# Decayed cumulative sum of a matrix product: the start of the kernel and the engine orders of its first 42 slots

## The chip, the cores and the metric

One Trainium2 chip, one of its cores. The metric is the device time of one execution in microseconds (us); nine runs of the kernel before are at hand, and one execution taken by the hardware profiler.

## The reference

`x` is 16 x 2048 x 1024, `w` 1024 x 1024 and `decay` 1024 long, all float32.

```python
def reference(x, w, decay):
    B, S, D = x.shape
    xw = x @ w
    out = np.zeros_like(xw)
    out[:, 0, :] = xw[:, 0, :].copy()
    for t in range(1, S):
        out[:, t, :] = decay[None, :] * out[:, t - 1, :] + xw[:, t, :]
    return out.astype(np.float32)
```

So there is a matrix product, and behind it, for each of the 1024 columns, a first-order recurrence along time.

## The kernel before

**Tiles and slots.** Time is cut into 64 chunks of 512 steps, four to a batch. Two chunks make a group, and the 1024 columns of `w` make 8 blocks of 128. A *slot* is one block for one group: an output of 128 columns x 1024 steps, with the columns on the partitions, made by 16 matmuls (8 parts `k` of the sum, 2 chunks) of 128 x 512 in bfloat16. The last group is run as single chunks, so there are 31 x 8 + 2 x 8 = 264 slots. The outputs lie in PSUM in a ring of three buffers `ps` (1024 float32 each) and two of half the size, `spare` and `spare1`. Slots 0 to 3 are made together, chunk 0 first, then chunk 1, in the three `ps` and the two spares (lines 547 to 564); the others one after the other (lines 567 to 594).

**Loading x.** A chunk comes as four DMAs, one for each quarter of the partitions, that GpSimd (POOL) issues and that turn float32 into bfloat16 on the way, into one of four `xb` buffers (`load`, line 101). Chunks 0 and 1 come in halves of 256 steps, four DMAs each (`load_half`; letters M0 to M3). The rest stand in the list `loads`, from which each letter L takes one; chunk c + 4 is put there when chunk c is turned.

**Turning x.** VectorE (DVE) transposes a chunk in blocks of 32 x 32, two bfloat16 at a time (`turn`, line 110; T, or its halves t and u; E for the eight pieces of chunks 0 and 1), into one of two `xw`. ScalarE (ACT) sorts the pairs apart into one of five `xt` (`part`, line 119; X and Y are the halves of a chunk). In chunks 0 and 1 there are pieces of a quarter of the sum and half the time, done by VectorE (F) or ScalarE (G).

**Loading w.** `w` comes in quarters (h, e): h is the half of the columns, e the even or odd rows. They land in `stage`, which lies in the two output buffers not needed yet, and are copied into `wsb` in eight pieces of two quarters for each h: `settle`, W on VectorE, w on ScalarE. W0 and W1 are k = 0 and 2, W2 and W3 k = 4 and 6, W4 to W7 the odd k of h = 0; W8 to W15 are h = 1. Quarter (0, 0) is loaded as float32 by SyncE's queue in two parts, at the very start and again at line 317 behind the decays. The others come by POOL's queue as bfloat16: U1, U2 and U3. The 8 DMAs in flight on a queue each have a semaphore of their own, and a ninth waits for the first of them.

**The recurrence of a slot.** There are two ways (`Tile`, line 136). *Unpaired*: VectorE scans all 1024 steps straight from PSUM (S, line 216). *Paired*: ScalarE copies the output out of PSUM (`copy`) and scales its odd-placed steps by the decay (`odd`), POOL adds them in (`join`), VectorE scans 512 steps with the squared decay (S, line 196), ScalarE scales that result (`even`) and POOL adds the rest (`fill`). In both the result `so` is transposed back by VectorE (B, line 253) into an output buffer `ot`, which SyncE stores when four slots are in it. P is copy, odd, zero and join together (p, g, z, j are the parts); C is even, fill and the saving of the last step (h, c, k). A slot's `ps` is free after its `odd` if paired, after its S if not. A slot is unpaired when its block n is 3 or 7, except that `flips` turns the choice round; with the list of before slots 0, 2, 3, 8, 11, 13, 16, 20, 21, 23, 25, 30, 32 and 39 of the first 42 are unpaired.

**What sets the order.** Each engine works through its instructions in the order of the program. That order is written out by hand as letters: `agenda[-99]` is the start, `agenda[s]` what is put behind the matmuls of slot s. For a slot with no entry `usual(s)` makes the order: P of s, S of s - 1, S of s if it is unpaired, C of s - 1, B of s - 2 (or s - 1), then the T, X and Y that `later` has for this slot, then one or two L. `later` puts T, X and Y of an odd chunk 7, 6 and 4 slots ahead of its first slot, of an even one 11, 10 and 8. In the kernel before, slots 0 to 41 and the last 20 are written out, and `usual` serves the 200 or so between. T14 and X13, Y13 are the first that come from `later`.

**Slots 8 and 9.** Chunk 2 is used ahead of chunk 3: step 8 makes both slots, chunk 2 of each and then chunk 3 of each (lines 577 to 585).

Before the first work on x, 27 matmuls of zeros run on TensorE (line 308).

Of the kernel before, what the change touches and what calls it, by code (L numbers as in the profile page):

```python
# [10 lines left out]
BF16 = mybir.dt.bfloat16  # L11
# [14 lines left out]
def kernel(  # L26
# [26 lines left out]
    nc = tc.nc  # L53
    pin = tc.keep_in_program_order
    B, S, D = x.shape
# [5 lines left out]
    K = CQ // P  # L61
    M = K // 2
    TL = 512
    NJ = TL // P
    NC = S // TL
    R = K // 2
# [32 lines left out]
    xt_of = {}  # L99
# [10 lines left out]
    def turn(c, j0=0, j1=NJ, m0=0, m1=M):  # L110
        if c not in xw_of:
            xw_of[c] = ring(sb, "xw", 2, [128, M, NJ, P, 2], BF16)
        src = xb_of[c][:, j0:j1].rearrange("p j c -> p (j c)").bitcast(FP32)
        dst = xw_of[c].rearrange("p m j i e -> p (m j i e)").bitcast(FP32)
        pin(nc.vector.transpose(  # L115
            out=dst.rearrange("p (m j i) -> p j m i", m=M, i=P)[:, j0:j1, m0:m1],
            in_=src.rearrange("p (j m c) -> p j m c", m=M, c=P)[:, :, m0:m1]))
# [143 lines left out]
    class Outlet:  # L261
# [7 lines left out]
        def store(self, b, t0):  # L269
# [3 lines left out]
            for i, q in enumerate((0, 2, 1, 3)):  # L273
# [7 lines left out]
    room = [ot_tile(2 * NJ).rearrange("p j c -> p (j c)") for _ in range(2)]  # L281
    size = M * CH
    stage = {(0, 0, 0): room[0][:, 0:size // 2],
             (0, 0, M // 2): room[0][:, size // 2:size],
             (0, 1, 0): room[0][:, size:size * 3 // 2].bitcast(BF16),
             (1, 0, 0): room[1][:, 0:size // 2].bitcast(BF16),
             (1, 1, 0): room[1][:, size // 2:size].bitcast(BF16)}
# [1 line left out]
    def load_w(queue, h, e, m0=0, m1=M):  # L289
        for q in range(NQ):  # L290
            pin(queue.dma_start(  # L291
                out=stage[h, e, m0][quad(q)].rearrange("p (m d) -> p m d", m=m1 - m0),
                in_=_ap(w, [[2 * D, P], [2 * P * D, m1 - m0], [1, CH]],
                        (q * CQ + m0 * 2 * P + e) * D + h * CH)))
# [18 lines left out]
    for q in range(NQ):  # L313
        pin(nc.sync.dma_start(
            out=rows[q * P:q * P + R],
            in_=_ap(decay, [[P, R], [CH, 2], [1, P]], q * CR)))
    load_w(nc.sync, 0, 0, M // 2, M)
    cols = const.tile([128, 2, P], FP32, name="cols")

    def load_half(i):  # L320
# [65 lines left out]
    slots += [([c], n) for c in groups[-1] for n in range(K)]  # L386
    tiles = []

    def turn_half(half):
        def act(c):  # L390
            if half == 0:
                turn(c, 0, NJ, 0, 2)
            else:
                turn_and_load(c, 2)
        return act

    def turn_and_load(c, m0=0):
        turn(c, 0, NJ, m0, M)
        if 2 <= c < nch - 4:
            loads.extend((c + 4, q) for q in range(NQ))  # L400

# [4 lines left out]
        "C": lambda s: tiles[s % len(slots)].complete(),  # L406
        "B": lambda s: tiles[s % len(slots)].back(),
        "T": turn_and_load,
        "t": turn_half(0),
        "u": turn_half(1),  # L410
        "X": lambda c: part(c, nc.scalar.copy, 0, 2),
        "Y": lambda c: part(c, nc.scalar.copy, 2, M),
        "x": lambda c: part(c, nc.vector.tensor_copy, 0, 2),
# [21 lines left out]
        "L": lambda i: load(*loads.pop(0)) if loads else None,  # L435
    }
    agenda = {
        -99: "M0 M1 U1 M2 M3 U2 U3 W0 w1 D W2 w3 E1 E0 G2 G3 F1 F0 E2 E3 G4 G5 F7 F6 W6 w7 W4 W5 E5 E4 G10 F11 G9 F8 E6 E7 L G12 F13 L G15 F14",
        0: "L W9 w11 L W8 W10 L",
        1: "S0 L",  # L440
        2: "L p1 z1",
        3: "L w13 S2 w15 k0 L w14 w12 g1",
        4: "L B0 k2 j1 B2 p4 L S1 L g4",
        5: "j4 t2 k1 h1 u2 L X2 c1 S3 Y2 z4 L",
        6: "L L B1 k3 p5 B3 p6 z5 z6 L",
        7: "g6 S4 g5 L j6 t3 h4 k4 u3 c4 X3 S6 L Y3 L T4 j5 h6 k6 p7 S5 z7 c6 g7",
        8: "",
        9: "d B4 k5 h5 j7",
        10: "X4 B6 c5 S8 Y4 L B5",
        11: "p9 L p10 S7 g9 B8 h7 j9 g10 T5",  # L450
        12: "k7 z9 c7 z10 j10 B7 X5 L S9",
        13: "L p12 S11 L h9 z12 Y5 c9 S10",
        14: "L g12 B11 h10 j12 B9 L S12 c10",
        15: "p14 S13 g14 L h12 j14 B10 c12",
        16: "p15 B13 L g15 B12 z14 z15 j15 S14 L",
        17: "S15 h14 c14 S16 h15 c15",
        18: "p17 B14 z17 L g17 L B15 k16 j17 B16",
        19: "z18 p18 S17 g18 T6 h17 j18 k17 c17",
        20: "T7 p19 z19 L g19 L X6 L B17 j19",
        21: "X7 S18 L S20 Y7 L S19",  # L460
        22: "k20 h18 k18 L Y6 S21 c18 k19 h19 B20 L",
        23: "k21 p22 c19 B18 g22 j22 B19 z22 L B21",
        24: "S22 S23 z24 k22 h22 c22",
        25: "p24 T8 k23 g24 j24 B23 X8 L",
        26: "L B22 L Y8 L S25 z26",
        27: "z27 p26 S24 g26 B25 h24 j26 T9 c24",
        28: "p27 g27 B24 L X9 j27 S26",
        29: "z28 L z29 p28 S27 L g28 L T10 h26 j28 Y9 c26",
        30: "S28 X10 B26 Y10 T11",
        31: "h28 S30 p29 c28 g29 h27 j29",  # L470
        32: "B28 X11 c27 S29 Y11 B30 B27",
        33: "p31 T12 g31 z31 h29 j31 c29 S32 X12",
        34: "p33 B29 g33 B32 k32 z33 Y12 j33",
        35: "S31 p34 z34 S33 h31 T13 h33 c31",
        36: "g34 k33 j34 p35 B31 g35 c33 S34",
        37: "j35 p36 B33 h34 z35 z36 S35 k34 g36 c34 k35 h35 j36 B34",
        38: "p37 z37 c35 S36 g37 j37 h36 B35 k36",
        39: "c36 p38 S37 g38 z38 B36 k37 h37 j38 c37 S38",
        40: "S39 h38 k38 c38 B37 p40 g40 z40 j40 k39 B38 B39 L L",
        41: "p41 g41 z41 j41 S40 h40 c40 L L",  # L480
        -20: "z-20",
        -19: "p-20 g-20",
        -18: "j-20 S-19 S-20 k-19 B-19",
# [15 lines left out]
        -2: "S-3 S-4",  # L499
        -1: "S-2 h-4 c-4 a-1 b-1 V",  # L500
    }
    flips = (0, 2, 7, 8, 13, 15, 16, 19, 20, 21, 25, 27, 30, 31, 32, 35, -19, -18, -16, -11, -8, -6, -3, -2)
    later = {}
    begun = {"T": 14, "X": 13, "Y": 13}
    for c in range(5, nch):
        first = c // 2 * K
        ahead = (7, 6, 4) if c % 2 else (11, 10, 8)
        for letter, a in zip("TXY", ahead):
            if c >= begun[letter]:
                later.setdefault(first - a, []).append(f"{letter}{c}")  # L510

    def usual(s):
        paired = [t.paired for t in tiles]
# [25 lines left out]
    for step, (g, n) in enumerate(slots):  # L539
        T = TL * len(g)  # L540
        left = step - len(slots)
        if n % R == 0:
            ns, nj = range(n, n + R), T // P
            outlets = [Outlet(ns, nj)]
        if left == -R:
            outlets = []
        if step == 0:
            heads = [ring(psp, "ps", 3, [128, T]) for _ in range(3)]
            firsts = [ps[:, 0:TL] for ps in heads] + [spares[0]]
            seconds = [ps[:, TL:T] for ps in heads] + [spares[1]]  # L550
            for j0, j1 in halves:
                for k in (0, 2, 4, 6):
                    for i in range(R):
                        matmul(firsts[i], i, k, xt_of[0], j0 * P, j1 * P)
            for k in (1, 3, 5, 7):
                for i in range(R):
                    matmul(firsts[i], i, k, xt_of[0])
            for k0 in range(0, K, 4):
                for i in range(R):
                    for k in range(k0, k0 + 4):  # L560
                        matmul(seconds[i], i, k, xt_of[1], 0, H * P)
            for i in range(R):
                for k in range(K):
                    matmul(seconds[i], i, k, xt_of[1], H * P, TL, H * P)
        if step < R:
            ps = heads[n] if n < 3 else tuple(spares)
        else:
            if step == K + 1:
                ps = nexts
            elif len(g) == 2 or n % R < 3:  # L570
                ps = ring(psp, "ps", 3, [128, T])
            else:
                ps = ring(psp, "spare", 1, [128, TL])
            todo = [(k, l) for k in range(K) for l in range(len(g))]
            if step < K:
                todo.sort(key=lambda kl: kl[0] % 2)
            elif step == K:
                todo = []
                nexts = ring(psp, "ps", 3, [128, T])
                for l in range(len(g)):  # L580
                    for i, both in enumerate((ps, nexts)):
                        for k in range(K):
                            matmul(both[:, l * TL:(l + 1) * TL], n + i, k, xt_of[g[l]])
            elif step == K + 1:
                todo = []
            if left == -1:
                ps = tuple(both[:, t:t + TL // 2] for t, both in zip(
                    (0, TL // 2), (ps, ring(psp, "ps", 3, [128, TL]))))
                for t, half in zip((0, TL // 2), ps):
                    for k in range(K):  # L590
                        matmul(half, n, k, xt_of[g[0]], t, t + TL // 2, t)
                todo = []
            for k, l in todo:
                matmul(ps[:, l * TL:(l + 1) * TL], n, k, xt_of[g[l]])
        tiles.append(Tile(g, n, ps, outlets))
        do = agenda.get(step, agenda.get(left) if left >= -20 else None)
        if do is None:
            do = usual(step)
        else:
            do = do.split()  # L600
            if left == -20:
                do = rest(step) + do
        perform(do)
# [29 lines left out]
```

## Time and profile before

| | |
|---|---|
| median of 9 runs | 913.1 us (912.2 to 913.79) |
| the profiled execution, its own time | 913.1 us |
| its span, first to last instruction | 911.2 us |
| TensorE (PE) busy | 897.7 us, 4195 matmuls |
| VectorE (DVE) busy | 831.0 us |
| ScalarE (ACT) busy | 675.7 us |
| GpSimd (POOL) busy | 649.2 us |
| mean granted clock of TensorE | 0.996 |
| one scan of 1024 steps from PSUM (L216) | 2261 ns, with the state of the group before 2321 ns |
| one scan of 512 steps (L196) | 1198 to 1280 ns |
| one transposition back (L253) | 1217 ns |
| one chunk turned (L115) | 2284 ns |
| half a chunk sorted (L123) | 1903 ns |
| copy, odd, even (L178, L164) | 1012, 693, 774 ns |
| one addition on POOL (L191, L241) | about 1300 ns |
| one load of x issued on POOL (L105) | 659 ns; landed 7.9 us after issue at the median |

The times of single instructions hold their start and end on the engine, which overlap the neighbours'; from one start to the next on a full engine it is some 0.1 us less. Queues land in order, so the space between two completions is what one DMA costs. TensorE's busy time is modelled from its starts; the share of the granted clock stands beside it. In what follows PE, DVE, ACT, POOL and SP are TensorE, VectorE, ScalarE, GpSimd and SyncE, and L with a number is a line of the kernel.

### The profile page before, as it was taken

How to read it: one execution, taken by the hardware profiler on the slowest of the kernel's cores; microseconds unless marked ns; L12 is line 12 of the kernel's file. 1: busy time of each engine (PE TensorE's matmuls, PEld its weight loads, DVE VectorE, ACT ScalarE, POOL GpSimd, SP SyncE). 2: the span in 40 equal slices, each digit the busy share in tenths (PEclk: the TensorE clock that was granted, in tenths of full speed). 3: DMA queues.
4: the chain of work that ended last, by engine and by line, in shares of the span. 5: the costliest groups of instructions: out<-in, count | busy, mean ns of one | idle time of the engine just before them, and what ended most of it. 6: DMA issues, size and time to landing. Idle time of an engine off the chain costs nothing.

```text
span 911.2 us, 12005 instructions
## 1 busy us (share of the span) xinstructions
PE 897.7 (99%) x4195; PEld 412.2 (45%) x4195; DVE 831.0 (91%) x622; ACT 675.7 (74%) x933; POOL 649.2 (71%) x745
## 2 busy tenths in 40 slices
PE   6999999999999999999999999999999999999997
PEld 3544444444444444444444444444444444444444
DVE  3899999899999999999999999999999999999998
ACT  2685797678778778777777787787787787787743
POOL 7778657787787777777777776777777877775632
PEclk8999999999999999999999999999999999999999
DMA  9999999999999999999999999999999999997868
GB/s 176 194 198 220 228 230 255 220 215 215 215 239 255 250 252 249 258 252 251 238 233 220 233 233 220 237 227 223 234 226 230 225 232 227 227 226 172 177 143 235
DMA packets 402604, 204.74 MB, mean 225 GB/s; under 512 B 8816, under 2 KB 401520, under 8 KB 402544
## 3 DMA queue, kind: packets, MB, share of 16 engines
q1 hardware_dynamic: 265520, 135.29, 60.5%
q0 software_dynamic: 137024, 68.70, 56.0%
q8 instruction: 32, 0.52, 0.2%
q14 instruction: 28, 0.23, 0.1%
HBM read 138.42 MB, written 134.22 MB: 299 GB/s over the span
## 4 chain that ended last, share of the span: by engine, by line
PE 95%; DVE 3%; DMA 1%; issue 1%; SPq 0%; DVEq 0%
PE ps L126 93%; DMA ot<-in_w_dram 1%; PE spare L126 1%; DVE so L216 1%; DVE xw L115 1%; DVE so L196 1%; DVE ot L253 0%; SPq L291 0%; PE spare L368 0%; DVE spare L340 0%; PE ps L368 0%; DVE h L372 0%; DVE xt L123 0%; DVEq L115 0%; DVE wsb L299 0%
## 5 line engine op out<-in xcount | busy, mean ns | idle before, releaser
L126 PE MATMUL ps<-xt,wsb 128*128 128x512 bf16 (+1 forms) x4092 | 880.2, 378 | 6.6 <-DVE xt L123 5.1
L126 PEld LDWEIGHTS <-wsb 128*128 128x128 bf16 x4152 | 407.3, 98 | 486.6 <-issue 7.4
L191 POOL TENSOR_TENSOR xs<-h,xs 128x512 f32<-128x512 f32 (+1 forms) x186 | 238.4, 1282 | 193.9 <-ACT h L164 89.2
L178 ACT COPY xs<-ps 128x1024 f32<-128x1024 f32 (+1 forms) x186 | 185.5, 999 | 165.9 <-PE ps L126 163.5
L253 DVE STREAM_TRANSPOSE ot<-so 128x1024 f32<-128x1024 f32 (+1 forms) x260 | 300.2, 1192 | 1.2 <-POOL so L241 0.5
L241 POOL TENSOR_TENSOR so<-h,xs 128x512 f32<-128x512 f32 (+1 forms) x186 | 237.9, 1279 | 45.5 <-ACT h L164 28.5
L123 ACT COPY xt<-xw 128x2048 bf16<-128x2048 bf16 (+1 forms) x132 | 239.8, 1825 | 9.6 <-DVE xw L115 9.6
L105 POOL DMA_DIRECT2D xb<-in_x_dram x264 | 173.6, 659 | 9.6 <-DMA xb<-in_x_dram 6.7
L164 ACT ACTIVATE h<-so,dec 128x512 f32<-128x512 f32 (+1 forms) x186 | 142.4, 766 | 24.2 <-DVE so L196 20.9
L115 DVE STREAM_TRANSPOSE xw<-xb 128x2048 f32<-128x2048 f32 (+2 forms) x72 | 146.9, 2047 | 3.0 <-DMA xb<-in_x_dram 3.0
L196 DVE TENSOR_TENSOR_SCAN so<-spare,keep,xs 128x512 f32<-128x512 f32 (+1 forms) x95 | 118.2, 1245 | 29.2 <-POOL xs L191 28.8
L196 DVE TENSOR_TENSOR_SCAN so<-spare,xs 128x512 f32<-128x512 f32 x87 | 106.3, 1221 | 25.3 <-POOL xs L191 22.6
L164 ACT ACTIVATE h<-ps,dec 128x512 f32<-128x512 f32 (+1 forms) x186 | 127.4, 686 | 0.0
L216 DVE TENSOR_TENSOR_SCAN so<-dec,ps 128x1024 f32<-128x1024 f32 x36 | 81.3, 2261 | 4.4 <-PE ps L126 3.8
L216 DVE TENSOR_TENSOR_SCAN so<-dec,keep,ps 128x1024 f32<-128x1024 f32 (+1 forms) x37 | 79.5, 2148 | 0.1
L245 ACT COPY keep<-so 128x1 f32<-128x1 f32 x136 | 25.6, 189 | 16.4 <-DVE so L216 12.2
L187 ACT COPY so<-keep 128x1 f32<-128x1 f32 x95 | 17.8, 191 | 1.2 <-DVE ot L253 1.2
L126 PE MATMUL spare<-xt,wsb 128*128 128x256 bf16 (+1 forms) x60 | 13.5, 336 | 0.0
L185 POOL MEMSET so<- 128x1 f32 x91 | 10.3, 115 | 3.3 <-DVE ot L253 3.3
L309 PE MATMUL spare<-idle 128*128 128x512 bf16 x27 | 8.5, 491 | 2.3 <-ACT idle L307 2.3
L299 DVE CAST wsb<-ot 128x512 bf16<-128x512 f32 x2 | 0.9, 428 | 9.6 <-DMA ot<-in_w_dram 9.6
L299 ACT CAST wsb<-ot 128x512 bf16<-128x512 f32 x2 | 1.2, 618 | 10.5 <-DMA ot<-in_w_dram 10.5
(32 smaller groups left out, 42.5 us busy)
## 6 DMA issues: line engine op xcount, KB each, us to landing
out_dram<-ot SPq DMA_DIRECT2D x248, 512.0 KB, 10.8
xb<-in_x_dram POOLq DMA_DIRECT2D x248, 256.0 KB, 7.9
out_dram<-ot SPq DMA_DIRECT2D x12, 256.0 KB, 4.1
xb<-in_x_dram POOLq DMA_DIRECT2D x16, 128.0 KB, 5.4
ot<-in_w_dram POOLq DMA_DIRECT2D x12, 128.0 KB, 5.7
ot<-in_w_dram SPq DMA_DIRECT2D x8, 128.0 KB, 5.1
out_dram<-xb SPq DMA_DIRECT2D x3, 256.0 KB, 2.2
out_dram<-h SPq DMA_DIRECT2D x1, 256.0 KB, 2.5
```

What stands on the lines that cost most here:

```text
L105: pin(nc.gpsimd.dma_start(out=xb_of[c][quad(q), j0:j1], in_=_ap(x, [[D, P], [P * D, j1 - j0], [1, CQ]], (b * S + t0 + j0 * P) * D + q * CQ)))
L115: pin(nc.vector.transpose(out=dst.rearrange("p (m j i) -> p j m i", m=M, i=P)[:, j0:j1, m0:m1], in_=src.rearrange("p (j m c) -> p j m c", ...
L123: pin(copy(out=xt_of[c][:, m0:m1, :, j0 * P:j1 * P], in_=src))
L126: pin(nc.tensor.matmul(out=ps[:, t0:t1] if ps.shape[1] >= t1 else ps, lhsT=wsb[:, k, n].rearrange("p q i -> p (q i)"), rhs=xt[:, k // 2, k ...
L164: pin(nc.scalar.activation(out=h, in_=src, func=mybir.ActivationFunctionType.Copy, scale=dec[:, self.n:self.n + 1]))
L178: pin(nc.scalar.copy(out=self.xs, in_=self.ps))
L191: pin(nc.gpsimd.tensor_tensor(out=odds, in0=self.g, in1=odds, op=ALU.add))
L196: pin(nc.vector.tensor_tensor_scan(out=so[:, 3:T + 2:2], data0=squares[-1][:, n:n + 1].to_broadcast([128, T // 2]), data1=self.xs[:, 1:T:2 ...
L216: pin(nc.vector.tensor_tensor_scan(out=so[:, t + 2:t + 2 + size], data0=dec[:, n:n + 1].to_broadcast([128, size]), data1=ps, initial=befor ...
L241: pin(nc.gpsimd.tensor_tensor(out=self.so[:, 2:T + 2:2], in0=self.h, in1=self.xs[:, 0:T:2], op=ALU.add))
L245: pin(nc.scalar.copy(out=self.keep, in_=self.so[:, self.T + 1:self.T + 2]))
L253: pin(nc.vector.transpose(out=outlet.ot[:, :, c0:c0 + P], in_=self.so[:, 2 + t0:2 + t0 + nj * P].rearrange("p (i t) -> p i t", t=P)))
```

## The change

The start and the first 42 slots are ordered anew. Quarter (0, 0) of `w` comes half by SyncE as float32 and half (U0) by POOL's queue as bfloat16, behind M0 and M1. `agenda` is written out for slots 0 to 16, and 17 to 41 follow `usual`. The first pieces of x are turned ahead of W2 and w3. `flips` leaves slots 0 and 1 unpaired besides the blocks 3 and 7. In slots 0 to 3 the halves of chunk 0 are used for k = 0 and 2 alone, and then whole chunks for k = 4, 6, 1, 3, 5, 7. Slot 8 is made by itself, chunk 2 first, then chunk 3, and slot 9 as any other. T of a chunk is one instruction throughout. The ring of four `xb` and the loading of chunk c + 4 at T of chunk c are in both kernels. The diff, with the orders of before left out:

```diff
     stage = {(0, 0, 0): room[0][:, 0:size // 2],
-             (0, 0, M // 2): room[0][:, size // 2:size],
+             (0, 0, M // 2): room[0][:, size // 2:size * 3 // 4].bitcast(BF16),
...
-    load_w(nc.sync, 0, 0, M // 2, M)
     cols = const.tile([128, 2, P], FP32, name="cols")
...
-    def turn_and_load(c, m0=0):
-        turn(c, 0, NJ, m0, M)
+    def turn_and_load(c):
+        turn(c)
         if 2 <= c < nch - 4:
             loads.extend((c + 4, q) for q in range(NQ))
...
-        -99: "M0 M1 U1 M2 M3 U2 U3 W0 w1 D W2 w3 E1 E0 G2 G3 F1 F0 E2 E3 G4 G5 F7 F6 W6 w7 W4 W5 E5 E4 G10 F11 G9 F8 E6 E7 L G12 F13 L G15 F14",
...
+        -99: "M0 M1 U0 U1 M2 M3 U2 U3 W0 w1 L E0 F0 G1 E1 L F2 D G3 E2 F4 L G5 W2 E3 F6 w3 G7 W4 W6 w5 w7 E4 F8 G9 E5 F10 G11 E6 F12 G13 E7 F14 G15 W8 W10 W9 W11",
+        0: "P0 L w15 w13",
+        1: "L L L S0 C0",
+        2: "L P2 P1 w12 S1 L L B0 B1 S2",
+        3: "w14 C2 T2",
+        4: "S3 P4 X2 Y2 T3 C1",
+        5: "",
+        6: "L L P5 L B3 L L S4 L S5 B2 C3 X3 Y3 C4 T4",
+        7: "P6 C5 S7 X4 S6",
+        8: "C7 C6 L d P8 B4 B7 B6",
+        9: "B5 P9",
+        10: "L S8 P10 C8 T5 X5 L S9",
+        11: "L L S11 L C9 Y4 S10 C10 B8",
+        12: "",
+        13: "B11 P12 B10 B9 Y5 S12 P13 C12",
+        14: "L P14 T6 S13 C13 L Y6 L",
+        15: "L S15 L S14 C14",
+        16: "B13 B12 B15 B14 P16 X6",
...
-    flips = (0, 2, 7, 8, 13, 15, 16, 19, 20, 21, 25, 27, 30, 31, 32, 35, -19, -18, -16, -11, -8, -6, -3, -2)
-    later = {}
-    begun = {"T": 14, "X": 13, "Y": 13}
+    flips = (0, 1, -19, -18, -16, -11, -8, -6, -3, -2)
+    later = {10: ["Y4"]}
...
-            if c >= begun[letter]:
-                later.setdefault(first - a, []).append(f"{letter}{c}")
+            later.setdefault(first - a, []).append(f"{letter}{c}")
...
-                for k in (0, 2, 4, 6):
+                for k in (0, 2):
                     for i in range(R):
                         matmul(firsts[i], i, k, xt_of[0], j0 * P, j1 * P)
-            for k in (1, 3, 5, 7):
+            for k in (4, 6, 1, 3, 5, 7):
                 for i in range(R):
                     matmul(firsts[i], i, k, xt_of[0])
...
-            if step == K + 1:
-                ps = nexts
-            elif len(g) == 2 or n % R < 3:
+            if len(g) == 2 or n % R < 3:
                 ps = ring(psp, "ps", 3, [128, T])
...
             elif step == K:
-                todo = []
-                nexts = ring(psp, "ps", 3, [128, T])
-                for l in range(len(g)):
-                    for i, both in enumerate((ps, nexts)):
-                        for k in range(K):
-                            matmul(both[:, l * TL:(l + 1) * TL], n + i, k, xt_of[g[l]])
-            elif step == K + 1:
-                todo = []
+                todo.sort(key=lambda kl: kl[1])
```

## The prediction

> **What bounds the kernel now.** I read the page first, then TensorE's waits, then the chain of waits, then the stages of the span.
>
> ```profile
> span 911.2 us, 12005 instructions
> PE 897.7 (99%) x4195; PEld 412.2 (45%) x4195; DVE 831.0 (91%) x622; ACT 675.7 (74%) x933; POOL 649.2 (71%) x745
> ...
> PEclk8999999999999999999999999999999999999999
> ```
> TensorE is the bound. Its waits (total, times, longest) are four in all, and the work starts only after the first:
>
> ```profile
> PE ps L126 <- DVE xt L123: 5.1, 1, 5.1
> PE spare L309 <- ACT idle L307: 2.3, 1, 2.3
> PE ps L126 <- DVE so L216: 1.3, 1, 1.3
> PE ps L126 <- ACT xt L123: 0.2, 1, 0.2
> ```
> The chain of waits (start, us) tells what the 5.1 and the 1.3 are:
>
> ```profile
> 6.23 6.99 DMA ot<-in_w_dram
> ...
> 13.69 1.31 DVE xw L115 x2
> ...
> 15.94 0.80 PE ps L126 x3
> ...
> 29.92 4.47 DVE so L216 x2
> ...
> 55.94 2.31 DVE so L216
> ...
> 58.29 823.78 PE ps L126 x3816
> ```
> SyncE's second load of w, issued at 6.23, lands at 13.22; W2 stands behind it in VectorE's order, the first turns of x (E1, E0, at 13.69) behind W2, and TensorE behind their copies. From 58.29 on TensorE never waits until the last transposes: 823.78 / 3816 = 0.2159 us a matmul, 3.454 a slot of 16. By stages (us, then busy time of PE, PEld, DVE, ACT, POOL, clock, DMA):
>
> ```profile
> 0.00:16.00 16.00, 8.57 (x28) 3.33 (x29) 3.97 (x12) 3.85 (x6) 10.59 (x22) 0.94 1.05 174
> 16.00:32.30 16.30, 16.30 (x112) 12.02 (x112) 9.85 (x20) 6.20 (x11) 12.48 (x22) 0.85 1.32 185
> 32.30:58.30 26.00, 24.55 (x115) 10.96 (x114) 25.89 (x21) 23.74 (x32) 20.59 (x25) 1.00 1.39 206
> 58.30:150.00 91.70, 91.70 (x425) 41.56 (x425) 91.66 (x64) 70.91 (x92) 61.41 (x69) 1.00 1.20 222
> ```
> Slots 0 to 3 take from 15.94 to 32.34 (16.4 us for 64 matmuls' work, 13.8 at full clock; the clock's records show half rate from 14.21 to 21.04). Slots 4 to 10 are 24.18 us of matmuls plus 1.77 of gaps before 58.29. VectorE is full from 30 to 150: whoever lets its first scan begin earlier moves everything. The slots from 42 on and the end are the same code in both, so only the start of slot 11 and any wait in slots 11 to 41 can change the time.
>
> **Edits worth nothing.** The four input buffers and the loads of chunk c + 4 stand in both kernels; that part of the title is no change. T2 and T3 in one piece cost 2.19 us from start to next start, as two halves do (37.67 to 39.94, 2.27). The flips leave 12 full scans in slots 0 to 41 where there are 14: VectorE's full scan takes 2.2, a paired one 1.14 (59.30 to 60.41, 64.86 to 66.02), so it saves 2.1 us; ACT gains 2 x (0.91 + 0.58 + 0.67) = 4.3 and POOL 2 x 2 x 1.24 = 5.0, spread over 145 us in which ACT was at 77% and POOL at 67%. Uncovered they would cost that much.
>
> **The start.** Removed: four loads on SyncE (2.54 us of issue, nothing behind them). Added: U0, four issues on POOL at 0.57 = 2.3 us. Behind them stand U1, M2 and so on, each of which waits for the landing eight loads before it, so the issue hides in that wait. The bytes read are the same. The completion events put U2 and U3 0.65 us apart; between 8.77 and 14.18 SyncE's four and M1's four landed, 5.4 us = 8 x 0.68. So U0 costs what it replaces, but it stands after M1. With M0 at 8.4 (before 8.77, shared with SyncE; bound 8.0 to 8.77) and 0.65 each: M1 11.0, U0 13.4 to 13.6, U1 15.7 to 16.2, M2 18.4, M3 21.1, U2 23.6, U3 26.2, chunk 2 (1.34 each) 31.6, chunk 3 37.0. Bound on the late side: the landings of before, M3 22.37, U2 24.98, U3 27.57, chunks 34.07 and 39.42. POOL's issues took 0.54 to 0.82 us each beside VectorE's work; four at 0.27 over the least are 1.1 us, which those same waits hide. [...]
>
> VectorE (E 0.64, F 0.43, W 0.29 from start to start): W0 6.3; E0 8.5, F0 to 9.6, E1, F2 to 10.7, D to 11.3 (0.66 before), E2 to 12.0, F4 12.4; W2 waits for U0: 13.8; E3 14.4, F6 14.9; W4, W6 behind U1: 16.3; E4 to F10 20.7, E6 to F14 23.4; W8, W10, W9, W11 behind U2: 24.9. ACT's G and w (0.6 each) run beside them, last G15 at 23.5.
>
> TensorE: the 27 warming matmuls end at about 10.5. k = 0 and 2, first half, 10.5 to 11.3; second half waits for F4: 12.4 to 13.2; k = 4 waits for F6: 14.95; then 24 matmuls x 0.216 to 20.1. Chunk 1, first half, 3.45 to 23.55; second half, slot 0 done at 24.4, all four at 27.1. S0 (flip 0: full, 2.2) starts at 24.9 behind W11 and frees its buffer at 27.1. **Slot 4 starts at 27.2, not 32.34: 5.1 us earlier.**
>
> The clock must stay full for this. In before TensorE rested from 10.5 to 15.94, and the next records show half clock; here the rests are 1.1 and 1.75 us. The nearer row is the one with a short rest: 1.3 idle before 58.29, clock 1.00 in that stage. I take full clock; rival 2 prices the other end. [...]
>
> **Slots 4 to 41.** New waits, each from rows: ACT does w15, w13 behind U3, then k0 behind S0 (27.1), P2 (copy 0.91, odd 0.58) to 28.7, w12 29.25, w14 29.8; slot 4's odd k waits 0.4 for w12. VectorE runs S0, S1, B0, B1 (1.13), S2, T2, S3 (2.5), T3 to 39.65 without rest, B3, S4, S5, B2, T4 to 46.4, S7 48.6. ACT: X2, Y2 (1.8 each) behind T2 to 38.7, P5 40.3, X3, Y3 behind T3 to 44.1: slot 8 starts at 41.35 and waits 0.2 for Y3 in its chunk 3 half; the removed trick (slots 8 and 9 on chunk 2 first) would have hidden it. Behind Y3 stand C4 and P6 on ACT: slot 6's buffer is free at 46.4, slot 9 waits 1.4 (45.0 to 46.4). Slot 10 needs S7 (48.6, has until 49.9). Slot 11 starts at 27.2 + 24.18 + 0.4 + 0.2 + 1.4 = 53.4. Before: 58.29. **Difference -4.9.**
>
> From there VectorE (S6, d, four B, S8, T5, S9, S11 at 62.1 against slot 14's 63.8; T6 at 68.9; S15 at 74.5 against slot 18's 77.6; T7 at 81.3; S19 at 89.1 against slot 22's 91.4) stays 1.3 to 3 us ahead of the buffer TensorE wants. Chunk 6's last load is issued at 60.4 (behind C8's add on POOL), chunk 7's at 74.2 (behind C13's); with the median of 7.9 us to landing, 68.3 and 82.1: T6 no wait, T7 0.8, inside the slack. What is late next is S19, and it has 2.2. After slot 24 VectorE needs 24.7 us for 8 slots of 27.6, and the lag shrinks.
>
> Sum against the profiled execution (913.1 around a span of 911.2; the median of the runs is 913.1 too): 913.1 - 4.9 = **908.2**. With the landings of before, S0 starts at 26.25, and T3 waits for chunk 3: 2.9 gained, 910.2. With M0 at 8.0 and no wait at slot 9: 906.5.
>
> **Rivals.**
> 1. *VectorE falls behind the loads (slower).* Place: T6 and T7, in a fixed order, with scans behind them that free TensorE's buffers. If loads need L us to land, T6 waits L - 8.5, chunk 7's issue slips as much, T7 waits L - 7.1 more; less the 2.2 of slack TensorE loses 2L - 17.8. It eats 4.9 + 1.8 at L = 12.2, the point from which the change is slower. For it: landings between 60 and 125 us took 4.3 to 14.7. Against: those loads were issued in batches with many ahead of them; here fewer are. At L = 13.4 (the load issued at 98.6): 9.0 lost, 917.2.
> 2. *The clock halves in the start.* From 14.95 to 21.04 at 0.432: 14 of 24 matmuls; the rest to 23.2; chunk 1 to 30.1, S0 at 27.6. Slot 4 is 2.9 later, the chain 2.8: 911.0. For: the half clock of before came after a rest in just this stage; against: that rest was three times as long.
> 3. *The start's gain is lost to waits (no change).* L between 10.4 and 12.2 costs 3 to 6.6: 911.3 to 914.8, say 913. For and against as in 1.
>
> **How the numbers follow.** About 0.2% (1.8 us) is what a measurement can tell from no change: 911.3 and 914.9 are the bounds. Forecast 0.49 (its own range 906.5 to 910.5), rival 1 0.27, rival 2 0.13, rival 3 0.11. Rival 2 lies at the bound and is split 0.09 faster, 0.04 same: faster 0.58, same 0.15, slower 0.27. The time is the forecast's, 908.2; the range runs from 906.5 to 917, which leaves the worst of rival 1 out.
>
> **What would show it.** First matmul of x near 10.5, rests of about 1 and 1.8 us before 15, clock 1.00 from 10 to 30, slot 4 near 27, a wait of TensorE for ACT's odd h or copy near 45 to 46.5, slot 11 near 53.4, and no wait after. Wrong if S0 starts after 28, if the clock is half at 15 to 21, or if VectorE waits for x at T6 or T7 and TensorE for a full scan soon after.

## The result

The changed kernel takes **908.51 us** (median of 9 runs, 908.02 to 910.12) against 913.24 us for the kernel before (29 runs). The ratio is 0.9951, with a 95% interval of 0.9943 to 0.9959: 4.7 us faster. The forecast was 908.2.

In the profiled execution the span went from 911.2 to 906.5 us. The page of the changed kernel, top and clock:

```profile
span 906.5 us, 12003 instructions
PE 896.3 (99%) x4187; PEld 410.3 (45%) x4187; DVE 828.3 (91%) x620; ACT 680.0 (75%) x940; POOL 655.3 (72%) x754
...
PEclk9999999999999999999999999999999999999999
```
Busy shares say nothing of the gain: TensorE is at 99% as before. In the line of the clock one digit differs, the first. TensorE's waits (total, times, longest):

```profile
PE spare L309 <- ACT idle L307: 2.3, 1, 2.3
PE ps L126 <- ACT wsb L299: 1.4, 1, 1.4
PE ps L126 <- DVE xt L123: 1.1, 2, 0.9
PE ps L126 <- DVE wsb L299: 0.6, 1, 0.6
PE ps L126 <- DVE so L216: 0.2, 1, 0.2
```
The wait of 5.1 us for the first piece of x is gone; two short ones for later pieces, 1.1 together, are left. A wait for w on ACT has come in its stead. The last row is slot 4's start, which waits for slot 0's scan. (These views count a wait from the modelled end of the matmul before. The waits that the text gives between two matmuls of full width are counted from start to start, less 0.216 us, which makes them 0.16 longer: 1.59 where the list has 1.4.) The chain of waits (start, us) shows where they lie:

```profile
21.93 5.64 DMA ot<-in_w_dram
...
27.67 1.14 ACT wsb L299 x2
...
28.90 0.91 ACT xs L178
29.81 0.59 ACT h L164
30.40 0.52 ACT wsb L299
...
30.96 46.97 PE ps L126 x216
...
89.49 2.27 DVE so L216
...
91.80 785.79 PE ps L126 x3640
```
The last part of w lands at 27.57. ACT copies it in w15 and w13, does slot 2's copy and odd (P2, from 28.90), then w12, and TensorE, which had begun slot 4 at 27.65, goes on with it at 30.96. After that the only waits of weight are 0.17 us at slot 9 (46.68) and 0.23 at slot 22 (91.80, for VectorE's full scan S19). By stages, the two in which the gain was made, in the kernel before and then in the changed one (us, then busy time of PE, PEld, DVE, ACT, POOL, clock, DMA):

```profile
10.00:20.00 10.00, 4.85 (x24) 3.08 (x23) 6.00 (x14) 3.56 (x7) 7.21 (x13) 0.71 1.35 199
20.00:30.00 10.00, 10.00 (x73) 7.22 (x72) 4.16 (x11) 2.90 (x5) 7.74 (x14) 0.95 1.27 185
```

```profile
10.00:20.00 10.00, 8.24 (x46) 4.18 (x44) 5.36 (x14) 3.71 (x7) 8.50 (x17) 1.00 1.31 181
20.00:30.00 10.00, 9.31 (x74) 6.98 (x72) 9.17 (x14) 4.60 (x9) 7.41 (x13) 1.00 1.32 195
```
Between 10 and 20 us TensorE starts 46 matmuls, where the kernel before started 24 at a clock of 0.71. Slot 0's scan starts at 25.33 (29.92 before), slot 4 at 27.65 (32.34), and slot 11 at 53.6 (58.29). The last product with w starts at 899.8 instead of 904.3. So the lead of 4.7 us is there at slot 11 and is kept to the end, but for the 0.23 us at slot 22.

### The profile page after: what moved, and what is told of

It reads as the page before. It is cut to its first block, busy times and chain, and to the rows that moved or that the text cites. A ratio compares the mean times of both kernels' runs of the same rounds, so it can differ in the third digit from the quotient of the medians.

```text
span 906.5 us, 12003 instructions
## 1 busy us (share of the span) xinstructions
PE 896.3 (99%) x4187; PEld 410.3 (45%) x4187; DVE 828.3 (91%) x620; ACT 680.0 (75%) x940; POOL 655.3 (72%) x754
## 4 chain that ended last, share of the span: by engine, by line
PE 95%; DMA 2%; POOL 1%; ACT 1%; issue 1%; DVE 0%; ACTq 0%; POOLq 0%
PE ps L126 94%; DMA ot<-in_w_dram 1%; POOL ot L291 1%; PE spare L126 1%; DMA xb<-in_x_dram 1%; POOL xb L105 0%; ACT xs L178 0%; POOL xs L191 0%; DVE so L216 0%; ACT xt L123 0%; ACT h L164 0%; ACT wsb L299 0%; POOL so L241 0%; PE spare L367 0%; PE ps L367 0%
## 5 line engine op out<-in xcount | busy, mean ns | idle before, releaser
L178 ACT COPY xs<-ps 128x1024 f32<-128x1024 f32 (+1 forms) x188 | 187.6, 998 | 148.0 <-PE ps L126 146.3
L115 DVE STREAM_TRANSPOSE xw<-xb 128x2048 f32<-128x2048 f32 (+1 forms) x70 | 147.4, 2105 | 6.4 <-DMA xb<-in_x_dram 6.4
L196 DVE TENSOR_TENSOR_SCAN so<-spare,keep,xs 128x512 f32<-128x512 f32 (+1 forms) x96 | 119.3, 1243 | 26.6 <-POOL xs L191 26.2
L196 DVE TENSOR_TENSOR_SCAN so<-spare,xs 128x512 f32<-128x512 f32 x88 | 107.4, 1220 | 26.3 <-POOL xs L191 23.7
L216 DVE TENSOR_TENSOR_SCAN so<-dec,ps 128x1024 f32<-128x1024 f32 x35 | 79.0, 2260 | 0.6 <-ACT h L164 0.6
L216 DVE TENSOR_TENSOR_SCAN so<-dec,keep,ps 128x1024 f32<-128x1024 f32 (+1 forms) x36 | 77.2, 2144 | 0.1
L126 PE MATMUL spare<-xt,wsb 128*128 128x512 bf16 (+1 forms) x58 | 12.3, 328 | 0.0
L291 POOL DMA_DIRECT2D ot<-in_w_dram x16 | 8.7, 541 | 2.7 <-DMA xb<-in_x_dram 0.9
L299 ACT COPY wsb<-ot 128x512 bf16<-128x512 bf16 x7 | 4.0, 616 | 5.5 <-DMA ot<-in_w_dram 5.5
```

The lines of the kernel that those rows point to most:

```text
L115: pin(nc.vector.transpose(out=dst.rearrange("p (m j i) -> p j m i", m=M, i=P)[:, j0:j1, m0:m1], in_=src.rearrange("p (j m c) -> p j m c", ...
L126: pin(nc.tensor.matmul(out=ps[:, t0:t1] if ps.shape[1] >= t1 else ps, lhsT=wsb[:, k, n].rearrange("p q i -> p (q i)"), rhs=xt[:, k // 2, k ...
L178: pin(nc.scalar.copy(out=self.xs, in_=self.ps))
L196: pin(nc.vector.tensor_tensor_scan(out=so[:, 3:T + 2:2], data0=squares[-1][:, n:n + 1].to_broadcast([128, T // 2]), data1=self.xs[:, 1:T:2 ...
L216: pin(nc.vector.tensor_tensor_scan(out=so[:, t + 2:t + 2 + size], data0=dec[:, n:n + 1].to_broadcast([128, size]), data1=ps, initial=befor ...
```

## The experiments

The question was which part of the change makes the 4.7 us: the order of the first turns, the load of w, the clock, or the orders of slots 0 to 41. Where nothing else is said, "against changed" is the difference to 908.51 us, and the ratio is to the kernel before, with its 95% interval. Times inside a kernel are those of one profiled execution. In four other kernels with the very same start (e7, e8, e9, e11) slot 4 begins at 27.97 to 28.32 where the changed kernel has 27.65, so some tenths in them mean nothing.

**e1_turn_late: the changed kernel with W2 and w3 ahead of the first turns.**

```diff
-        -99: "... W0 w1 L E0 F0 G1 E1 L F2 D G3 E2 F4 L G5 W2 E3 F6 w3 G7 ...",
+        -99: "... W0 w1 W2 w3 L E0 F0 G1 E1 L F2 D G3 E2 F4 L G5 E3 F6 G7 ...",
```


> The changed kernel with W2 and w3 put back ahead of E0; loads and all else as changed. Theory 1 (the gain is the order of VectorE's first turns): E0 waits for U0 (12.5), the first matmul comes near 14.0, slot 0's scan 2.1 us later than 25.3, slot 4 near 29.8; slots 4 to 10 win back little, so 1.5 to 2.5 us slower than the changed kernel, 910.0 to 911.0. If TensorE's rest of some 3 us halves the clock, 2 us more, up to 913. Theory 2 (the gain is the lighter load of w): the order is worth nothing, 908.5.

Measured 912.89 us, ratio 0.9998 (0.999 to 1.0007): the whole gain is gone. First matmul at 14.11, scan of slot 0 at 29.75, slot 4 near 32. The stages of this kernel, columns as above:

```profile
10.00:20.00 10.00, 5.46 (x25) 2.99 (x24) 6.95 (x17) 4.75 (x8) 8.69 (x17) 0.73 1.29 180
20.00:30.00 10.00, 10.00 (x67) 6.48 (x66) 4.35 (x11) 3.00 (x5) 7.27 (x13) 0.93 1.32 196
```
The clock is at 0.73 again; its records show half rate from 14.59 to 21.42, after a rest of TensorE of 3.1 us. The loss is at the top of the range named for a halved clock. Theory 2, that the load of w is the gain, falls: the lighter load is still in this kernel.

**e5_late_warm: the same, with TensorE kept busy until the first matmul.**

```diff
-    for _ in range(27):
+    for _ in range(44):
```


> The changed kernel with W2 and w3 ahead of E0, as in e1_turn_late, and 44 matmuls of zeros instead of 27, so that TensorE does not rest before the first matmul at 14.1. Parts the two prices in e1_turn_late's loss of 4.4 us. Theory: the late turns cost 2.0 us by themselves and the half clock the other 2.4, so 910.0 to 911.0. Rival: the half clock is all of it (the later start is covered by waits for data), 908.5 to 909.2; or it is nothing, 912.5 or more.

Measured 911.77 us, ratio 0.9992 (0.9983 to 1.0001). The clock stays full (1.00 in 10 to 20 us), and 1.1 us of the 4.4 come back. So the late turns cost 3.3 us by themselves and the clock 1.1. That lies between the theory and the second half of its rival, outside every range named. Slot 0's scan starts at 27.64, 2.3 us later than in the changed kernel. Slot 9 is 2.3 us later too (49.01): it waits 1.24 us there, for ACT's odd, while slot 4's wait is down to 0.43. Slot 22 (0.58 at 94.49) adds 0.35, and the last product with w starts 2.7 us later. The other 0.6 of this execution's loss lie behind the last product, where none of the changes is.

**e4_warm: the kernel before, with the clock kept up.**

```diff
-    for _ in range(27):
+    for _ in range(51):
```


> The kernel before with 51 matmuls of zeros instead of 27, so that TensorE does not rest before 15.9. Prices the clock alone: if half clock cost slots 0 to 3 their 2.5 us and the data is there, slot 4 starts near 30.0 and the time is 910.5 to 911.5. If the data sets that stage, the clock is worth under 0.5 us: 912.7 or more.

Measured 910.72 us, ratio 0.9975 (0.9966 to 0.9985), 2.3 us faster than the 913.02 of the kernel before in the same comparison, with nothing else changed. The clock is full, the first matmul comes at 15.945 as before, slot 0's scan at 27.46 instead of 29.92, and the waits behind are the old ones (0.33 and 1.45). So in the kernel before the half clock alone cost 2.3 us.

**e2_turn_early: the kernel before with the first turns ahead of W2 and w3.**

```diff
-        -99: "... W0 w1 D W2 w3 E1 E0 G2 G3 F1 F0 E2 E3 G4 G5 F7 F6 W6 ...",
+        -99: "... W0 w1 E0 F0 G1 E1 F2 D G3 W2 w3 E2 F4 G5 E3 F6 G7 W6 ...",
```


> The kernel before with one change: E0, F0, G1, E1, F2, G3 and D ahead of W2 and w3 in the order of the start; SyncE's load stays. Theory 1: first matmul near 11, rest of 2 us before k = 4, clock full, scan of slot 0 near 25.9, slot 4 near 28.2 against 32.3; the old orders behind it keep 3 to 4 us of that: 909 to 910.3. Theory 2 (load of w): the order gives nothing by itself, 913.

Measured 910.17 us, ratio 0.9976 (0.9968 to 0.9985). First matmul at 10.0, full clock in spite of a rest of 2.3 us, slot 0's scan at 24.95, 5.0 us earlier than before. Only 2.9 us arrive at the end (913.02 beside it), 3.5 in the profiled execution. Up to slot 5's scan S5 the old orders keep nearly all of the lead: S6 starts at 43.31 (48.06 before), S5 at 46.83 (51.43). But S5 takes 2.28 us where it took 1.18 before (first row before, second e2):

```profile
51.43 1.18 DVE L196 TENSOR_TENSOR_SCAN so<-squares,xs 128x512 f32<-128x512 f32 x1
...
46.83 2.28 DVE L196 TENSOR_TENSOR_SCAN so<-squares,xs 128x512 f32<-128x512 f32 x1
```
POOL had begun an addition, slot 6's fill, at 46.74, of which 1.20 us were left when S5 began; the last section has the other scans of this form that began during one. VectorE runs without a wait from there to the full scan of slot 8, and TensorE waits for that one in front of slot 11:

```profile
PE ps L126 <- DVE so L216: 2.5, 1, 2.5
```
Slot 11 starts at 54.79 after this wait, 3.5 us earlier than before.

**e3_sync_load: the changed kernel with SyncE's second load of w.**

```diff
-             (0, 0, M // 2): room[0][:, size // 2:size * 3 // 4].bitcast(BF16),
+             (0, 0, M // 2): room[0][:, size // 2:size],
...
+    load_w(nc.sync, 0, 0, M // 2, M)
...
-        -99: "M0 M1 U0 U1 M2 M3 U2 U3 ...
+        -99: "M0 M1 U1 M2 M3 U2 U3 ...
```


> The changed kernel with the second part of quarter (0, 0) loaded as float32 by SyncE again, behind the decays. Theory 1: landings as in the kernel before (M1 14.2, M3 22.4, U3 27.6); half 1 of chunk 0 starts near 15.4, slot 0's scan near 26.5, slot 4 near 29.1, less waiting for w12 in slot 4: 0.5 to 1.5 us slower than the changed kernel, 909 to 910, and up to 912 if the rest from 11.9 to 15.4 halves the clock. Theory 2 (load of w): the whole gain goes, 913.

Measured 911.45 us, ratio 0.999 (0.9981 to 0.9998), 2.9 us against changed. M1 lands between 10.92 and 13.77 instead of 9.16 and 11.20, the second half of chunk 0 starts at 15.12 instead of 12.91, TensorE rests 3.9 us and the clock is 0.67 between 10 and 20 us (half from 13.49 to 20.32). So the load does matter: SyncE's four DMAs land between M0 and M1's end, M1 ends 2.57 us later, and the clock falls in the rest of 3.9 us that this makes. How much of it is their place ahead of M1 and how much their size (128 KB each, where U0's write 64) was not tried apart. With a full clock 0.5 to 1.5 was expected; the part of the clock was not measured apart here either.

**e6_old_orders and e10_old_start: the two halves of the change by themselves.** The first is the kernel before with the changed start (loads, first turns, order of `k` in slots 0 to 3). The second is the changed kernel with the start of before.

```diff
e6, on the kernel before:
...
-    load_w(nc.sync, 0, 0, M // 2, M)
...
-        -99: "M0 M1 U1 M2 M3 U2 U3 W0 w1 D W2 w3 E1 E0 ...
+        -99: "M0 M1 U0 U1 M2 M3 U2 U3 W0 w1 L E0 F0 G1 E1 L F2 D ...
...
-                for k in (0, 2, 4, 6):
+                for k in (0, 2):
...
e10, on the changed kernel: the same lines the other way round
```
W8 to W11 stand only once in each: e6 leaves them out of the start, as the old orders have them in slot 0, and e10 puts them at the end of the start.

> The start of the changed kernel (loads, first turns, order of k in slots 0 to 3) with everything of the kernel before behind it: its orders of slots 0 to 41, its flips, slots 8 and 9 on chunk 2 first. Theory 1 (the orders are worth little, the start is the gain): slot 4 near 27.5, slot 11 near 53.5 to 54.8 with the wait for the full scan of slot 8 at 1.5 to 2.7 us, 908.5 to 910. Theory 2 (a good part of the gain is in the orders): 911 or more.

> The other half of e6_old_orders: the start of the kernel before (SyncE's second load, W2 and w3 first, order of k) with the orders, flips and slot 8 of the changed kernel. Theory 1 (the parts work only together; the orders by themselves give next to nothing, since the start sets slot 0's scan at 29.9): slot 4 near 32.3, slot 9 waits 1.4, slot 11 near 57.9, 912.4 to 913.4. Theory 2 (the orders are the gain): 909.5 to 911.

| | orders of before | orders of changed |
|---|---|---|
| start of before | 913.24 | 913.07 (e10), ratio 1.0001 (0.9992 to 1.001) |
| start of changed | 914.21 (e6), ratio 1.0014 (1.0005 to 1.0023) | 908.51, ratio 0.9951 (0.9943 to 0.9959) |

Neither half gives anything alone, and the start alone is 1 us slower than before. The theory for e10 held. For e6 the first theory missed (908.5 to 910), and of the second only its "or more" holds: a kernel slower than before was not foreseen. In e6 slot 0's scan starts at 25.84, 4.1 us earlier than before, yet slot 11 starts at 59.05, 0.8 later. S1, the first paired scan, is only 1.5 us earlier already (35.02, before 36.57), and POOL's timeline shows why (start, us, instruction, idle before and its releaser):

```profile
30.49 0.64 POOL L105 DMA_DIRECT2D xb<-in_x_dram  x1 [0.71 <-DVE so L216]
31.55 0.64 POOL L105 DMA_DIRECT2D xb<-in_x_dram  x1 [0.41 <-DMA xb<-in_x_dram]
32.94 0.64 POOL L105 DMA_DIRECT2D xb<-in_x_dram  x1 [0.76 <-DMA xb<-in_x_dram]
33.69 1.30 POOL L191 TENSOR_TENSOR xs<-h,xs 128x512 f32<-128x512 f32 x1
```
The old order puts loads of x on POOL ahead of slot 1's join (33.69), and each load waits for the landing eight loads before it (0.41 and 0.76 us in these rows). These landings did not come earlier with TensorE: the last part of w lands at 28.62 in e6 and at 27.57 in the kernel before, while slot 0's scan starts 4.1 us earlier. In the kernel before the join ran at 34.65, behind ACT:

```profile
34.65 1.28 POOL L191 TENSOR_TENSOR xs<-h,xs 128x512 f32<-128x512 f32 x1 [2.37 <-ACT keep L245]
```
So an earlier start by 4.1 us moves it by only 1.0. The mixture makes it a little worse: the changed start has three loads L where the old one has two, so 28 loads stand ahead of this join instead of 27. By S6 the lead is 1.3 us (46.76, before 48.06), and S6 itself loses 2.0 more, again with an addition of POOL (slot 4's fill, begun at 46.68) under way:

```profile
46.68 1.29 POOL L241 TENSOR_TENSOR so<-h,xs 128x512 f32<-128x512 f32 x1
...
46.76 3.15 DVE L196 TENSOR_TENSOR_SCAN so<-squares,xs 128x512 f32<-128x512 f32 x1
...
56.70 2.30 DVE L216 TENSOR_TENSOR_SCAN so<-dec,keep,ps 128x1024 f32<-128x1024 f32 x1
```
VectorE works without a wait from S6 to the full scan of slot 8 at 56.70 (55.94 before). TensorE waits 3.25 us for that, and the clock is halved from 59.7 to 63.1, some 1.7 us more (3.4 us at half rate). With an S6 of usual length the wait would have been some 1.3 us, no longer than the 1.3 in front of slot 11 in the kernel before, where the clock stayed full (1.00 from 32.3 to 150 us); so I estimate that this one scan costs 3.7 us here. The ten executions of e6 agree: three at a mean clock of 0.999 or more take 912.3 to 912.5 us, seven at 0.997 or 0.998 913.9 to 915.3. The stages of the profiled one, with TensorE's busy time, clock, DMA and GB/s:

```profile
50.00:60.00 10.00, 6.55 (x29) 0.99 1.30 215
60.00:70.00 10.00, 9.95 (x39) 0.84 1.27 188
```

**e12_join_first: e6 with slot 1's odd and join ahead of the loads.**

```diff
-        2: "L p1 z1",
-        3: "L w13 S2 w15 k0 L w14 w12 g1",
-        4: "L B0 k2 j1 B2 p4 L S1 L g4",
+        2: "L p1 g1 z1 j1",
+        3: "L w13 S2 w15 k0 L w14 w12",
+        4: "L B0 k2 B2 p4 L S1 L g4",
```


> e6_old_orders with slot 1's odd and join (g1, j1) ahead of the loads on POOL and of w12 to w15 on ACT. In e6_old_orders POOL does j1 at 33.7, behind four loads that wait for landings, and S1 waits 2.5 us for it, so the start's gain is gone by S1. Theory: S1 at 32.6, chain 2 us earlier, slot 11 near 57: 911.5 to 912.5. Rival (later waits in the old orders take it back): 913.5 or more.

Measured 914.08 us, ratio 1.0012 (1.0003 to 1.0021): nothing won, as the rival had it. S1 did move, to 31.69, and S4 to 40.96 (43.18 in e6). But S6 waits for its own join, which has loads in front of it too:

```profile
43.76 0.65 POOL L105 DMA_DIRECT2D xb<-in_x_dram  x1 [1.91 <-issue]
44.42 1.30 POOL L191 TENSOR_TENSOR xs<-h,xs 128x512 f32<-128x512 f32 x1
```
S6 follows at 45.76, 1.0 us earlier than in e6, and takes 3.16 us; slot 4's fill, begun at 45.67, is under way again. Slot 11 keeps the 1.0 us (58.05), but TensorE has waited 3.25 us for it again, and the clock halves again (0.91 in 50 to 60 us, 0.92 in 60 to 70). So the join of slot 1 is one of several places, and mending one only shows the next. The traces show two ways in which the old orders lose the lead: loads ahead of joins, and additions of POOL that run into a scan. No run moved the additions by themselves. The loss also depends on the start: e2_turn_early keeps 4.6 us of its lead up to S5 under the same orders (its last part of w lands at 26.77, that of e6 at 28.62).

**e7_trick: the changed kernel with slots 8 and 9 on chunk 2 first.** The lines that the change removed are put back.

```diff
             elif step == K:
-                todo.sort(key=lambda kl: kl[1])
+                todo = []
+                nexts = ring(psp, "ps", 3, [128, T])
+                for l in range(len(g)):
+                    for i, both in enumerate((ps, nexts)):
+                        for k in range(K):
+                            matmul(both[:, l * TL:(l + 1) * TL], n + i, k, xt_of[g[l]])
```


> The changed kernel with slots 8 and 9 on chunk 2 first, then both on chunk 3, as in the kernel before. By the prediction the trick would hide the wait for Y3 (0.2). Theory now: slot 9's buffer comes free only at 46.5 (ACT's odd of slot 6), and the trick wants it at 44.8, so TensorE waits 1.7 there: 909.5 to 910.3. Rival (the trick helps): 908.2 to 908.5.

Measured 910.2 us, ratio 0.9973 (0.9964 to 0.9983): 1.7 us slower than changed. TensorE waits 2.29 us at 47.33 for slot 9's buffer, which ACT frees with the second of these lines:

```profile
45.66 1.03 ACT L178 COPY xs<-ps 128x1024 f32<-128x1024 f32 x1
46.56 0.72 ACT L164 ACTIVATE h<-ps,dec 128x512 f32<-128x512 f32 x1
```
So removing the trick is a gain of 1.7 us in the changed kernel. The prediction had booked it as a small loss.

**e9_late_loads: the price of the rival in which VectorE falls behind the loads.**

```diff
-        11: "L L S11 L C9 Y4 S10 C10 B8",
+        11: "S11 C9 Y4 S10 C10 B8 L L L",
```


> The changed kernel with the three loads of slot 11 moved behind C10 and B8 on POOL's queue; the first of them is the last of chunk 6. Prices the prediction's first rival: T6 waits some 4 us longer (issue 65.7 instead of 60.9), chunk 7's issue slips with it and T7 waits too, and VectorE's scans of slots 15 and 19 come too late. By the rival's sum every us of this is lost to TensorE, as there is a wait of 0.2 at slot 22 already: 4 to 7 us slower than the changed kernel, 912.5 to 915.5. If TensorE's three buffers cover it: under 1 us, 908.5 to 909.5.

Measured 912.26 us, ratio 0.9992 (0.9983 to 1.0001), 3.75 us against changed. VectorE's waits between 24 and 110 us, in the changed kernel and then in e9:

```profile
DVE xw L115 <- DMA xb<-in_x_dram: 2.1, 3, 1.3
```

```profile
DVE xw L115 <- DMA xb<-in_x_dram: 4.0, 2, 3.8
```
T6 waits 3.8 us instead of 1.3 and starts 3.8 us later (74.34 instead of 70.55): 2.5 us by its wait, and 1.2 because the scan before it is later too (69.22 instead of 68.02; it waits 0.8 for POOL's join). TensorE's waits for full scans rise from 0.2 to 3.5 us in all (2.0 at slot 18, 1.58 at slot 22). The result is a little under the range, but the mechanism is there: 3.8 us at T6 cost 3.75 in the end, so none of it is covered.

**e8_new_orders and e11_new_orders: two tries at a faster version.** Both take the changed kernel's orders of slots 0 to 11 and put P2 ahead of w12 to w15, P6 ahead of C4, and T4 behind S7.

```diff
e8:
-        0: "P0 L w15 w13",
-        1: "L L L S0 C0",
-        2: "L P2 P1 w12 S1 L L B0 B1 S2",
-        3: "w14 C2 T2",
+        0: "P0 L",
+        1: "L L L S0",
+        2: "L P2 P1 w12 w13 w14 w15 C0 S1 L L B0 B1 S2",
+        3: "C2 T2",
...
-        7: "P6 C5 S7 X4 S6",
-        8: "C7 C6 L d P8 B4 B7 B6",
+        7: "P6 C4 C5 S7 C7 L L B4 T4",
+        8: "S6 L d P8 X4 C6 L B7 B6",
...
e11, where it differs:
+        7: "P6 C4 C5 S7 T4 S6",
+        8: "C7 L L d P8 B4 C6 L L X4 B7 B5 B6",
```


> The changed kernel with a new order in slots 0 to 11: P2 ahead of w12 to w15, then C0 (takes away slot 4's wait of 1.6); P6 ahead of C4, T4 and X4 behind S7 and P8 (frees the buffers of slots 9 and 10 sooner); two loads of chunk 6 two slots earlier (T6 does not wait 1.3). Theory: slot 4 without a wait, slot 9 at 45.8 instead of 46.7, no wait at 91.8: 907.0 to 907.8. Rival (the buffers behind bind at once, nothing is won): 908.3 to 909.

> A second try at a version faster than both: the changed kernel with P2 ahead of w12 to w15 and C0 (takes away slot 4's wait of 1.6), P6 ahead of C4, S7 ahead of T4, X4 behind P8 and C6, B5 ahead of B6, chunk 6's loads earlier. Theory: slot 9 starts at 45.8 instead of 46.7, T6 does not wait, no wait at slot 22: 907.2 to 908.2. Rival (as in e8_new_orders, ACT waits for VectorE's B4 in slot 8's zero and the buffers come later): 909 to 911.

Measured 910.38 us for e8 (ratio 0.9975, 0.9967 to 0.9984) and 910.59 us for e11 (0.9971, 0.9959 to 0.9983): faster than the kernel before, 1.9 and 2.1 us slower than the changed one. Slot 4's wait did go in both, and slots 8 and 9 then wait 1.0 us together in e8 and 1.2 in e11. In e8 VectorE waits 2.0 us for POOL's fills in front of B4 and B6, and TensorE 0.84 and 1.23 us at slots 13 and 14 behind that. In e11 TensorE waits 1.59 us at slot 12 (58.42) and 1.42 at slot 22 (94.37), the latter behind a T7 that waits 2.7 us for x. For e11 the rival held (909 to 911). e8 lies above both of its ranges, the rival's 908.3 to 909 too: the new order did not only win nothing, it lost 1.9 us. That slot 4's wait in the changed kernel only stands in for later ones is what I read from this; it was not tried by itself. No version here beats the changed kernel.

## Why the prediction was right, and where it was off

The time, the sign and the chain of causes were right. Step by step:

- *The bound and where the change acts.* Right: the lead was made by slot 11 (53.6, forecast 53.4) and kept. The end of the kernel and the slots from 42 on did not move.
- *Landings.* M0 8.48 (8.4), M1 11.20 (11.0). **U0 was mis-sized**: I gave its four DMAs 0.65 us each, and they took 0.33 (landed 11.54 to 12.54, forecast 13.4 to 13.6): they write 64 KB each, and U1's first three, which write 128, took 0.65. What that won was lost again at two single DMAs: U1's last came 1.7 us after the one before it (16.22), and U3's third 1.8 (27.32). U3 ended at 27.57 (26.2), chunk 2 at 32.80 (31.6), chunk 3 at 38.13 (37.0).
- *The start.* First matmul 10.97 (10.5), S0 25.33 (24.9), slot 4 at 27.65 (27.2). The rests of TensorE were 0.96 and 0.30 us (1.1 and 1.75), with a third of 0.8 us at 16.69, for W4 and W6 behind U1, that the sum did not have; the clock stayed full. The clock is a quarter to a half of the matter: it halved with rests of 3.1 (e1) and 3.9 us (e3), and that cost 1.1 us in e1 (against e5) and 2.3 in the kernel before (e4). Rival 2 had priced it at 2.8.
- *Slot 4's wait.* Forecast 0.4, measured 1.59. It follows from U3: w15 began at 27.67, not at 26.2.
- *Slots 8 and 9.* Forecast 0.2 and 1.4, measured 0.17 in all. The buffer of slot 9 came free at 46.5, as forecast (46.4); TensorE arrived later, held up in slot 4. The sum of waits from slot 4 to 11, 2.0, was nearly right (1.8) with its terms wrongly shared. That slot 11 came within 0.2 us of the forecast is not all luck: slot 9's buffer, free when forecast, held slot 9 to that time whichever wait came before. That the other errors nearly cancelled, the early U0 and the late U3 above all, is luck.
- *The trick of slots 8 and 9.* Wrong: "would have hidden it". e7 shows that it costs 1.7 us here. I looked at the wait for Y3 and not at what the trick needs in its place, the buffer of slot 9 1.7 us sooner.
- *T6, T7, S19.* T6 waited 1.29 us (0), T7 0.35 (0.8), and S19 took all of its 2.2 us of slack and 0.23 more. The change stands at the edge of rival 1, and e9 shows its price.
- *The edits worth nothing.* Only half right. The flips and the orders by themselves are worth nothing (e10), but the sum credited the whole gain to the start, and with the orders of before this start gives 914.2 us (e6). Early turns alone, under the orders of before, give 910.2 (e2). How much the new orders are worth in general stays open: in e6 an estimated 3.7 us, and in e2 1.1, lie in a single scan that met an addition of POOL.

## What to carry to other kernels

When the first useful instruction waits, look first at what stands ahead of it on its own engine's queue, and at whether the bounding engine loses its clock by its rest, as it did here with rests of 3.1 (e1) and 3.9 us (e3); e1 differs from the changed kernel by an order alone, and the two by 4.4 us. An earlier start only pays as far as the orders behind it can follow: an instruction with work ahead of it that waits for landings can stay nearly where it was, as slot 1's join in e6 did (1.0 us earlier of 4.1), and one that does come earlier can meet another engine's work that it missed before, as the scans of slots 5 and 6 did in e2 (2.28 us, before 1.18) and e6 (3.15 us, before 1.24). Before booking a removed trick as a loss, ask which buffer it needed and when.

## What the runs showed of the hardware

- In the kernel before the record of the granted clock starts at 7.39 and changes at 14.21 and 21.04, which is 2 and 4 times 3.413 us later; in the changed kernel it starts at 8.08 and changes at 905.79, 263 times 3.413 us later. Half rate lasted 6.83 us in the kernel before, in e1 (from 14.59) and in e3 (from 13.49), and 3.4 us in e6 (from 59.7). In the 3.413 us ahead of half rate TensorE had been without a matmul for 2.19 us in e3, 2.76 in e6, 2.81 in e10, 2.94 in e1, 3.08 in e12 and all 3.41 in the kernel before; stretches that held 1.91 us without one in e2 and 1.80 in e8 left the clock full. In e3 the rest was 2.2 us old when the clock fell; in e2 a rest of 2.5 us lay across the end of a stretch (1.65 and 0.88), and the clock stayed full. That the place of a rest counted there beside its length is read from these two; no run moved a rest by itself. In the kernel before the first half of the time at half rate still held a rest, to 15.94, and the second, 17.63 to 21.04, held none.
- In the changed kernel the four DMAs of U0, which write 64 KB each, landed 0.33 us apart, and the first three of U1, 128 KB each, 0.65: half the bytes, half the time. Both turn float32 into bfloat16.
- A scan of 512 steps (L196) whose squared decay lies in SBUF (`squares` in its row) took 1.17 to 1.23 us when no addition of POOL was running at its start (37 in the fourteen traces). The 19 that began during one took up to 3.16, longer in those where more of it was left: with 0.16 us left 1.24 (before), with 0.47 left 1.55 (changed), with 1.00 left 2.08 (e1, e10), with 1.20 left 2.28 (e2) and 3.15 (e6, e12). Once the letter d has put the squared decay into PSUM (`spare`), none of 2482 took over 1.29, though 1551 began with 0.3 us or more of an addition to go. Only e6 and e12 lose more than was left of the addition, 0.8 us more, and why is open. That POOL's addition is the cause is read from these rows; no run moved it.
